# Token normalisation of both FFNs in a segment of its own, transposes through four PSUM banks, and a reset of buffer ages in the mixer

## The chip, the core and the metric

One NeuronCore of a Trainium2 chip runs the whole block for 1024 tokens of width 1024 in float32. The metric is device microseconds of one execution; before the change the median of three runs is 2161.04 us (2158.54 to 2163.19). The engines are TensorE (PE, with its weight loads as PEld), VectorE (DVE), ScalarE (ACT), GpSimd (POOL) and SyncE, whose queue SP issues the DMAs.

## What is computed

```python
x = x + 0.5 * swiglu_ffn(x, ffn1_norm, ...)      # d_ff = 2816
h = rms_norm(x, mix_norm); P = h @ w_in          # 4944 columns
ya = dsa_attention(...)                          # indexer scores, top 256 keys, softmax
yb = mlstm_branch(...)                           # causal conv, chunkwise scan
x = x + (sigmoid(ga) * (ya @ w_proj_a) + sigmoid(gb) * (yb @ w_proj_b)) @ w_out
x = x + 0.5 * swiglu_ffn(x, ffn2_norm, ...)

def swiglu_ffn(x, g, w_gate, w_up, w_down):
    h = rms_norm(x, g)
    return (silu(h @ w_gate) * (h @ w_up)) @ w_down
```

## The kernel before

**Products.** Every float32 operand is split into a high and a low part, and each product is three matmuls (`mm3`, lines 658 to 660). The gate and up projections use a seven-product scheme over 2x2 blocks (Strassen's form): the normalised, transposed tokens are combined into seven operands T0 to T6 of four 128x512 panels each (a high and a low part per panel), and the weight blocks are combined in the same way, on the fly, by `Pairs._prep` (lines 253 to 303: sums on DVE at L280 to L291, the high part on ACT at L297, the low part on DVE at L298). `gate_up` (line 911) walks 11 column pairs p and seven products q: first (0,0), (0,1), (1,0), (1,1), then the other five of p = 0 in the order 5, 4, 6, 2, 3, then all seven of each further p. One (p, q) is 24 matmuls of 512 columns: gate and up, four panels, three parts.

**The prologue.** `operands` (line 846) is a generator that makes T0 to T6; `gate_up` advances it just ahead of the product that needs the operand: T0 and T1 ahead of (0,0), T5 ahead of (0,1), T4 ahead of (1,0). It goes so:

- tokens 0 to 3 (128 each) are normalised by `norm` (line 759): a square with row sum on ACT into a scratch buffer (L763), a scale on DVE (L664), a power on POOL (L665), a multiplication on DVE (L765) into a buffer `xn`;
- for k = 0 to 7, `turned` (line 769) transposes column block k of the four tokens into one PSUM bank (four PE transposes, L773), and `put_turned` (line 835) reads the bank three times: high part on ACT (L841), low part on DVE (L842), a plain copy on ACT (L844) into one of four buffers `b1`. This gives T0 (k = 0 to 3) and T1 (k = 4 to 7);
- the four `xn` buffers are freed; tokens 4 to 7 are normalised in place; eight more `turned` calls (each read once by ACT, L878) and DVE subtractions (L879, L880) give T5, then T4 (`put2`, `split`: L790, L791), T6 (L894), T2 and T3 (L905).

**Buffers.** SBUF is cut into segments of 1024-column pages with the program's own allocator: a `Segment` tracks 64-column units, an `Arena` chooses among segments. `find` (line 89) takes, among free places, the one freed longest ago (the highest `freed` mark in it is the lowest of all), or the lowest address when `keep` is set. A buffer that was freed in program order may still be read on the chip; its next writer then waits for that reader. Scratch buffers, `xn`, `b1`, the early weights (two pages in total) and evicted results all come from the arena `ar`, in an FFN the segments `plain` (nine pages) and `more` (two). `segment(tag, ...)` (line 621) replaces a segment by a fresh one, whose first writer waits for all users of the old one. The segment `h0` (eight pages) is empty at the start of both FFNs until T5 and T4 are put there.

**PSUM.** Eight banks. `psA` gives banks 0 and 1, `psB` (line 605) alternates between 2 and 3, `psS` alternates between the pairs 4-5 and 6-7. `turned` takes its bank from `psB`. `turned` is also used by the mixer's `late_tokens` and `early_tokens` (lines 1050 and 1073).

**Order.** The code's order gives priorities; the framework's planner then fixes one order per engine from modelled durations, and on the chip each engine runs its list in that order. The second FFN follows `merge` (line 2079), whose last step `accumulate` (line 794) finishes the tokens one by one: 24 matmuls per token (L805 to L809), then the residual addition on DVE (L810). The second FFN's normalisation of a token can begin when that is done. The mixer lies between the FFNs, from about 640 to 1491 us: projections (pumped between other work), indexer scores, top-k (`topk`, a background generator), the mLSTM, attention and the merge. Its buffers come from the same arena, first with `plain`, later with `more`, `extra`, `spare` and `rawx`.

Of the kernel before, what the change touches and what calls it, by code (L numbers as in the profile page):

```python
# [59 lines left out]
class Buf:  # L60
# [4 lines left out]
    def __init__(self, seg, off, n):  # L65
        self.seg, self.off, self.n = seg, off, n
        self.f = seg.t[:, off:off + n]
        self.r = self.f.bitcast(F32R)
# [509 lines left out]
class Block:  # L578
    def __init__(self, tc, pools, a):
        self.tc, self.nc, self.a = tc, tc.nc, a  # L580
        self.sb, self.ps, self.dr = pools
        self.ar, self.rr, self.own = Arena(), Arena(), {}
        self.plain("plain", "more")
        self.round("round", "spare", "extra")
        for t in ("raw", "rawx", "side"):
            self.segment(t, None)
        self.whole_raw = True
        self.w = Weights(self, 0, 0)
        self.bg = ()
        self.due = [0, 0]  # L590

        self.psum = self.ps.tile([P, 4096], F32, name="psum", bufs=1)
        self.turn, self.turnB, self.turnS = 0, 2, 4
        self.last = None


# [24 lines left out]
    def segment(self, tag, arena):  # L621

        old = self.own.pop(tag, None)
        if old:
            assert not any(old.used), tag
            for a in (self.ar, self.rr):
                if old in a.segs:
                    a.segs.remove(old)
        self.own[tag] = Segment(self.sb, tag, PAGES[tag])
        if arena:  # L630
            arena.segs.append(self.own[tag])

    def close(self, tag):

        for a in (self.ar, self.rr):
            if self.own[tag] in a.segs:
                a.segs.remove(self.own[tag])
# [130 lines left out]

    def turned(self, xn, k):

        ps = self.psB()
        for i in range(4):
            self.nc.tensor.transpose(ps[:, i * P:(i + 1) * P], xn[i].f[:, k * P:(k + 1) * P], self.ident)  # L773
        return ps
# [47 lines left out]
    def put(self, q, j, src, tag):  # L822

        hi, lo = self.take(tag, 512), self.take(tag, 512)
        self.split(hi.r, lo.r, src)
        self.T[q][j] = (hi, lo)

    def put2(self, q, i, src, tag):

        hi, lo = self.take(tag, 1024), self.take(tag, 1024)  # L830
        self.split(hi.r, lo.r, src)
        for j in range(2):
            self.T[q][2 * i + j] = hi.part(j * 512, 512), lo.part(j * 512, 512)
# [12 lines left out]
    def operands(self, xs, gain, spill=None):  # L846


        nc, ar, v = self.nc, self.ar, self.nc.vector
        T = self.T = {q: [None] * 4 for q in range(7)}  # L850
        put, put2 = self.put, self.put2
        xn = []
        for t in range(4):
            n = ar.alloc(1024)
            self.norm(xs[t], n)
            xn.append(n)
        if spill:
            for t in range(8):
                spill(t)
        b1 = [ar.alloc(1024) for _ in range(4)]  # L860
        for k in range(8):
            self.put_turned(k // 4, k % 4, xn, k, gain, "swap", b1[k // 2].f[:, k % 2 * 512:k % 2 * 512 + 512])
            if k == 3:
                yield 0
        for n in xn:
            n.free()
        yield 1
        for t in range(4, 8):
            self.norm(xs[t], xs[t])
        b11, b21 = b1[:2], b1[2:]  # L870
        t1, t2, b22 = [], [], []
        for i in range(2):
            two = [self.take("side", 1024) for _ in range(2)]
            n = ar.alloc(1024)
            for j in (2 * i, 2 * i + 1):
                c = slice(j % 2 * 512, j % 2 * 512 + 512)
                for b, k in zip(two, (j, 4 + j)):
                    nc.scalar.activation(b.f[:, c], self.turned(xs[4:8], k), AF.Copy, scale=gain[:, k:k + 1])  # L878
                v.tensor_tensor(two[0].f[:, c], two[0].f[:, c], b11[i].f[:, c], ALU.subtract)  # L879
                v.tensor_tensor(n.f[:, c], two[1].f[:, c], two[0].f[:, c], ALU.subtract)  # L880
                put(5, j, n.f[:, c], "h0")
            t1.append(two[0])
            b22.append(two[1])
            t2.append(n)
        yield 5
        for i in range(2):
            put2(4, i, t1[i].f, "h0")
            t1[i].free()
        yield 4
        for x in xs:  # L890
            x.free()
        self.segment("h1", None)
        for i in range(2):
            v.tensor_tensor(b11[i].f, t2[i].f, b11[i].f, ALU.subtract)  # L894
            put2(6, i, b11[i].f, "h1")
            b11[i].free()
        yield 6
        for i in range(2):
            put2(2, i, b22[i].f, "h1")
            b22[i].free()  # L900
        yield 2
        self.segment("side", None)

        for i in range(2):
            v.tensor_tensor(b21[i].f, b21[i].f, t2[i].f, ALU.subtract)  # L905
            put2(3, i, b21[i].f, "side")
            b21[i].free()
            t2[i].free()
        yield 3
# [139 lines left out]

    def late_tokens(self, xs, spill):  # L1050

        nc, v, gain = self.nc, self.nc.vector, self.g_mix
        self.segment("h1", None)
        self.segment("side", None)
        self.T = {q: [None] * 4 for q in range(7)}
        for t in range(4, 8):
            spill(t)
            self.norm(xs[t], xs[t])
        self.b12, self.b22 = [], []
        for i in range(2):  # L1060
            b12, b22 = self.take("side", 1024), self.take("side", 1024)
            for j in (2 * i, 2 * i + 1):
                c = slice(j % 2 * 512, j % 2 * 512 + 512)
                self.put_turned(2, j, xs[4:8], 4 + j, gain, "h1", b22.f[:, c])
                nc.scalar.activation(b12.f[:, c], self.turned(xs[4:8], j), AF.Copy, scale=gain[:, j:j + 1])
            n = self.ar.alloc(1024)
            v.tensor_tensor(n.f, b22.f, b12.f, ALU.subtract)
            self.put2(6, i, n.f, "h1")
            n.free()
            self.b12.append(b12)  # L1070
            self.b22.append(b22)
# [1041 lines left out]
    def run(self, x, out):  # L2113
        nc, ar = self.nc, self.ar
# [81 lines left out]
            self.close(t)  # L2196
        self.pump_past((GATES[2], 3))
        self.plain("more", "extra", "spare")
        self.staged(self.gates())
        self.bg = [self.topk(js, share) for js, share in zip(((2, 3, 4, 5), (6, 7)), self.tk)]  # L2200
        self.mlstm_begin()
# [28 lines left out]
            nc.sync.dma_start(xs[t].f, d_x[t])  # L2230
        pairs = Pairs(self, a["ffn2_w_gate"][0], a["ffn2_w_up"][0])
        self.merge(yaT, xs, pairs)
        self.segment("side", None)
        self.segment("h0", None)
        self.segment("swap", None)
# [49 lines left out]
```

## Time and profile before

| | us |
|---|---|
| median of 3 runs | 2161.04 |
| the profiled execution, whole | 2156.2 |
| its span in the profile | 2154.5 |
| PE busy in the span | 2067.5 (96%) |
| DVE busy | 1632.2 (76%) |
| ACT busy | 1040.8 (48%) |
| POOL busy | 381.2 (18%) |

Times in the profile count from the start of the span. "Idle before" is the time in which an engine stood still ahead of an instruction, with the engine, buffer and line that released it. PEclk is the granted TensorE clock as a share of full speed: 1.00 is 2.4 GHz, 0.50 is 1.2 GHz. A busy PE is not PE at its peak: matmuls overlap, and at half clock a slow matmul counts as busy too, so the pitch from start to start is what tells PE's speed.

### The profile page before, as it was taken

To read this page: it belongs to the slowest core of one execution; us is meant where nothing else is said; L and a number is where in the kernel's file an instruction comes from. 1 tells how busy PE (TensorE), PEld (TensorE's weight loads), DVE (VectorE), ACT (ScalarE), POOL (GpSimd) and SP (SyncE) were. 2 spreads that over 40 slices of the span, in tenths; PEclk is the share of its full clock that TensorE was granted. 3 is DMA by queue.
4 is the path that set the end of the run, shared out by engine and by line. 5 is a ranking of instruction groups with operands and counts; after the bars stand their busy time and mean duration, and the time that the engine had idled before them with its cause. 6 is when DMAs were issued, how large, how long until landed. Compare 5 with 4: busy or idle time off the path is not lost.

```text
span 2154.5 us, 27729 instructions
## 1 busy us (share of the span) xinstructions
PE 2067.5 (96%) x9397; PEld 1686.8 (78%) x9397; DVE 1632.2 (76%) x2806; ACT 1040.8 (48%) x1928; POOL 381.2 (18%) x391
## 2 busy tenths in 40 slices
PE   6999999999999999999998999899899999999999
PEld 5788787888887778677777787777688888888887
DVE  6987887678855885988899689665786667669964
ACT  7332233344446664965885578323633333334442
POOL 1000000000303224434445545221000000000300
PEclk9999999999999999999999999999899999999999
DMA  5379994393522324456775222612243333277341
GB/s 181 124 245 291 280 289 153 132 364 125 168 68 92 90 72 120 133 167 178 226 224 164 93 74 70 249 59 88 68 143 108 105 101 113 98 258 276 96 142 40
DMA packets 275466, 326.76 MB, mean 152 GB/s; under 512 B 20236, under 2 KB 185724, under 8 KB 275324
## 3 DMA queue, kind: packets, MB, share of 16 engines
q1 hardware_dynamic: 275324, 324.99, 46.5%
q8 instruction: 74, 1.21, 0.2%
q14 instruction: 68, 0.56, 0.1%
HBM read 224.23 MB, written 100.70 MB: 151 GB/s over the span
## 4 chain that ended last, share of the span: by engine, by line
PE 45%; DVE 10%; ACT 3%; DMA 2%; issue 2%; POOL 0%; SPq 0%; DVEq 0%; ACTq 0%; POOLq 0%
PE psum L658 12%; PE psum L660 12%; PE psum L659 12%; PE psum L1983 1%; DVE plain L1476 1%; PE psum L805 1%; PE psum L809 1%; PE psum L807 1%; DVE h L791 1%; PE psum L1365 1%; PE psum L2038 1%; PE psum L2037 1%; PE psum L1366 1%; ACT plain L1502 0%; ACT round L408 0%
## 5 line engine op out<-in xcount | busy, mean ns | idle before, releaser
L658 PE MATMUL psum<-h,round 128*128 128x512 f32 x656 | 261.8, 400 | 4.2 <-DVE plain L976 1.6
L659 PE MATMUL psum<-h,round 128*128 128x512 f32 x656 | 259.5, 396 | 1.1 <-DVE h L791 0.8
L660 PE MATMUL psum<-h,round 128*128 128x512 f32 x656 | 259.1, 395 | 0.3 <-DVE round L298 0.3
L545 POOL TENSOR_TENSOR swap<-swap,h 128x1024 f32<-128x1024 f32 x12 | 32.9, 2773 | 1014.8 <-DVE h L531 1014.8
L409 POOL TENSOR_TENSOR round<-raw,round 128x512 fp32r<-128x512 f32 x108 | 149.4, 1392 | 155.7 <-ACT round L408 122.1
L658 PEld LDWEIGHTS psum<-h,round 128*128 128x128 f32 x656 | 124.3, 190 | 33.9 <-DVE plain L976 2.0
L660 PEld LDWEIGHTS psum<-h,round 128*128 128x128 f32 x656 | 123.9, 189 | 27.9 <-issue 1.8
L659 PEld LDWEIGHTS psum<-h,round 128*128 128x128 f32 x656 | 124.2, 189 | 26.9 <-DVE h L791 1.3
L658 PE MATMUL psum<-swap,round 128*128 128x512 f32 x328 | 131.6, 406 | 9.9 <-ACT plain L1452 2.6
L660 PE MATMUL psum<-swap,round 128*128 128x512 f32 x328 | 129.9, 397 | 1.2 <-POOL round L409 1.2
L659 PE MATMUL psum<-swap,round 128*128 128x512 f32 x328 | 130.5, 398 | 0.1
L1476 DVE TENSOR_SCALAR_CACHE_REDUCE plain<-plain 128x384 bf16<-128x384 f32 (+1 forms) x124 | 100.3, 808 | 2.5
L297 ACT ACTIVATE round<-plain 128x512 fp32r<-128x512 f32 x75 | 46.8, 630 | 102.4 <-PE psum L659 80.6
L790 ACT ACTIVATE round<-plain 128x512 fp32r<-128x512 f32 x72 | 45.1, 631 | 102.2 <-PE psum L659 90.2
L658 PE MATMUL psum<-h,extra 128*128 128x512 f32 x200 | 80.2, 402 | 6.2 <-ACT h L790 4.9
L658 PEld LDWEIGHTS psum<-swap,round 128*128 128x128 f32 x328 | 63.2, 193 | 27.4 <-ACT plain L1452 3.0
L791 DVE TENSOR_TENSOR round<-plain,round 128x512 fp32r<-128x512 f32 x72 | 55.9, 780 | 37.6 <-ACT round L790 37.3
L408 ACT ACTIVATE round<-raw 128x512 fp32r<-128x512 f32 x108 | 66.4, 622 | 33.4 <-PE psum L659 20.6
L659 PE MATMUL psum<-h,extra 128*128 128x512 f32 x200 | 79.5, 397 | 2.2 <-DVE h L791 2.2
L658 PE MATMUL psum<-h,spare 128*128 128x512 f32 x200 | 78.8, 395 | 1.3 <-DVE plain L976 1.3
L660 PE MATMUL psum<-h,extra 128*128 128x512 f32 x200 | 79.0, 395 | 0.0
L659 PE MATMUL psum<-h,spare 128*128 128x512 f32 x200 | 78.4, 392 | 0.0
(753 smaller groups left out, 5972.5 us busy)
## 6 DMA issues: line engine op xcount, KB each, us to landing
plain<-d_a SPq DMA_DIRECT2D x154, 256.0 KB
d_a<-plain SPq DMA_DIRECT2D x131, 256.0 KB
raw<-in_ffn_w_gate_dram SPq DMA_DIRECT2D x44, 512.0 KB
raw<-d_s SPq DMA_DIRECT2D x74, 256.0 KB
h<-in_ffn_w_down_dram SPq DMA_DIRECT2D x66, 256.0 KB
plain<-in_w_in_dram SPq DMA_DIRECT2D x32, 512.0 KB
d_s<-plain SPq DMA_DIRECT2D x64, 256.0 KB
raw<-in_w_in_dram SPq DMA_DIRECT2D x53, 256.0 KB
```

The source lines that it names most:

```text
L297: k.nc.scalar.activation(hi.r.rearrange("p (k c) -> p k c", k=4), src, AF.Copy)
L408: self.done_A = k.nc.scalar.activation(hi.r, raw.f, AF.Copy).ins
L409: k.nc.gpsimd.tensor_tensor(lo.r, raw.f, hi.f, ALU.subtract)
L545: k.nc.gpsimd.tensor_tensor(x(th, dh), x(th, dh), u, ALU.add)
L658: mm(ps, lhs[0], rhs[0], start=start, stop=False, skip_group_check=more)
L659: mm(ps, lhs[0], rhs[1], start=False, stop=False, skip_group_check=more)
L660: mm(ps, lhs[1], rhs[0], start=False, stop=stop, skip_group_check=more)
L790: self.split_A = self.nc.scalar.activation(hi, src, AF.Copy).ins
L791: self.nc.vector.tensor_tensor(lo, src, hi.bitcast(F32), ALU.subtract)
L805: mm(ps[:, n:n + 512], ah, wh[:, n:n + 512], start=j == 0, stop=False)
L807: mm(ps[:, n:n + 512], ah, wl[:, n:n + 512], start=False, stop=False)
L1476: v.tensor_scalar(s.junk[:, :s.width[j]], s.sc[j], s.cand[:, j:j + 1], None, ALU.is_ge, ALU.add, accum_out=s.cnt[:, j:j + 1])
```

## The change

In both FFNs the four `xn` buffers come from `h0` instead of the arena, and `h0` is replaced by a fresh segment once they are freed. While the flag `wide` is set (from the start to the mixer's `late_tokens`, and again after `merge`), `turned` goes round banks 0 to 3 instead of 2 and 3. In the mixer, just ahead of the gates, the top-k and the mLSTM, `level()` sets the age mark of every unit of every segment to zero, so that `find` takes the first free place by address as long as there is one not used since. Nothing that is computed changes.

```diff
         self.psum = self.ps.tile([P, 4096], F32, name="psum", bufs=1)
-        self.turn, self.turnB, self.turnS = 0, 2, 4
+        self.turn, self.turnB, self.turnS, self.turnT = 0, 2, 4, 3
+        self.wide = True
         self.last = None
...
+    def level(self):
+
+        for s in self.own.values():
+            s.freed = [0] * len(s.freed)
...
     def turned(self, xn, k):
 
-        ps = self.psB()
+        if self.wide:
+            self.turnT = (self.turnT + 1) % 4
+            ps = self.bank(self.turnT)
+        else:
+            ps = self.psB()
...
         for t in range(4):
-            n = ar.alloc(1024)
+            n = self.take("h0", 1024)
             self.norm(xs[t], n)
             xn.append(n)
...
         for n in xn:
             n.free()
         yield 1
+        self.segment("h0", None)
         for t in range(4, 8):
             self.norm(xs[t], xs[t])
...
     def late_tokens(self, xs, spill):
 
+        self.wide = False
...
         self.pump_past((GATES[2], 3))
         self.plain("more", "extra", "spare")
+        self.level()
         self.staged(self.gates())
...
         self.merge(yaT, xs, pairs)
+        self.wide = True
         self.segment("side", None)
```

## Rows read from the trace of the kernel before

**Rows 1.** The page: the span, and the busy time of each engine.

```profile
span 2154.5 us, 27729 instructions
PE 2067.5 (96%) x9397; PEld 1686.8 (78%) x9397; DVE 1632.2 (76%) x2806; ACT 1040.8 (48%) x1928; POOL 381.2 (18%) x391
```

**Rows 2.** Windows: length, busy us (count) by engine, PEclk, DMA share, GB/s.

```profile
13.47:57.63 44.16, 38.27 (x164) 29.92 (x165) 33.15 (x53) 36.69 (x61) 3.56 (x4) 0.88 0.40 130
1491.59:1545.84 54.25, 42.50 (x170) 31.93 (x171) 33.12 (x52) 36.19 (x58) 4.11 (x5) 0.81 0.17 59
1540.00:1545.00 5.00, 4.40 (x10) 3.51 (x11) 5.00 (x7) 1.56 (x3) 0.00 (x0) 0.50 0.00 0
1650.00:1700.00 50.00, 50.00 (x222) 41.42 (x221) 33.81 (x54) 15.39 (x25) 0.00 (x0) 1.00 0.32 105
```

**Rows 3.** The same view of both prologues, transposes alone (L773; PE, PEld).

```profile
1491.59:1545.84 54.25, 10.99 (x58) 7.63 (x58) 0.81 0.17 59
13.47:57.63 44.16, 9.54 (x56) 7.69 (x56) 0.88 0.40 130
```

**Rows 4.** Timeline at the second FFN's start: start, us, what, [idle before <-releaser].

```profile
1482.96 1.22 DVE L810 SCALAR_TENSOR_TENSOR h<-psum,h 128x1024 f32<-128x1024 f32 x1 [0.87 <-PE psum L809]
...
1490.97 0.61 PE L809 MATMUL psum<-more,side 128*128 128x512 f32 x2
...
1491.67 1.06 ACT L763 ACTIVATE more<-h 128x1024 f32<-128x1024 f32 x1 [0.94 <-issue]
...
1494.48 0.65 PE L773 MATMUL psum<-ident,plain 128*128 128x128 f32 x2 [2.89 <-DVE plain L664]
...
1495.69 0.80 PE L658 MATMUL psum<-swap,round 128*128 128x512 f32 x1 [0.56 <-ACT swap L841]
...
1501.40 0.40 PE L659 MATMUL psum<-swap,round 128*128 128x512 f32 x1
...
1502.10 0.60 PE L773 MATMUL psum<-ident,plain 128*128 128x128 f32 x4
1502.46 0.48 PE L659 MATMUL psum<-swap,round 128*128 128x512 f32 x1
```

**Rows 5.** The same timeline, between the second FFN's two token halves.

```profile
1518.75 0.60 PE L773 MATMUL psum<-ident,plain 128*128 128x128 f32 x4
1519.06 1.06 ACT L763 ACTIVATE plain<-h 128x1024 f32<-128x1024 f32 x1 [4.04 <-PE psum L773]
...
1519.16 0.69 DVE L280 TENSOR_TENSOR plain<-raw 128x512 f32<-128x512 f32 x1 [4.88 <-PE psum L773]
...
1536.25 0.80 PE L658 MATMUL psum<-h,extra 128*128 128x512 f32 x1 [2.90 <-ACT h L790]
...
1540.60 0.80 PE L659 MATMUL psum<-h,extra 128*128 128x512 f32 x1 [2.19 <-DVE h L791]
```

**Rows 6.** DVE groups from 1494 to 1567 us: count, busy, mean ns, idle before.

```profile
L842 DVE SCALAR_TENSOR_TENSOR swap<-psum,par,swap 128x512 fp32r<-128x512 f32 x8 | 5.9, 749 | 14.1 <-ACT swap L841 14.1
```

**Rows 7.** The chain of waits, second FFN: start, us, what.

```profile
1544.63 4.43 DVE h L791 x5
...
1559.76 4.50 DMA rawx<-in_ffn_w_up_dram
```

**Rows 8.** Timeline of the first FFN's prologue.

```profile
32.67 1.06 ACT L763 ACTIVATE plain<-h 128x1024 f32<-128x1024 f32 x1 [0.81 <-PE psum L773]
...
44.02 1.97 PE L773 MATMUL psum<-ident,h 128*128 128x128 f32 x8 [2.39 <-ACT side L878]
```

**Rows 9.** Waits of PE on L878; then L844 by line: ns min/median/max.

```profile
PE psum L773 <- ACT side L878: 4.3, 6, 2.4
...
L844 ACT ACTIVATE plain<-psum,par x16: 672/689/730, 19.9 to 1513.7; 128x512 f32<-128x512 f32 x16
```

**Rows 10.** The mixer from 850 us: busy by engine, and PE's longest wait.

```profile
850.00:1450.00 600.00, 561.59 (x2760) 454.72 (x2761) 494.47 (x1082) 402.08 (x876) 260.66 (x275) 0.98 0.47 149
...
PE psum L2037 <- DVE h L1997: 6.4, 4, 2.8
```

## The prediction

> **What bounds the kernel now.** The page comes first [rows 1]: PE is busy for 2067.5 of 2154.5 us, so 87 us of idle PE is all that reordering can win, plus what PE loses while its clock is down. The windows say where that sits. In steady state (1650 to 1700 us) 222 matmuls take 50 us, a pitch of 0.225 us. The two prologues stand out [rows 2]. From 13.47 to 57.63 us PE finishes 164 instructions, from 1491.59 to 1545.84 us 170, at a mean clock of 0.88 and 0.81. Of these, 56 and 58 are transposes [rows 3], and four of those take 0.36 us of PE time when warm (1502.10 to 1502.46) [rows 4]. Without idling, at full clock, the first FFN's stretch would need 108 x 0.225 + 56 x 0.09 = 29.3 us of its 44.2, and the second's 112 x 0.225 + 58 x 0.09 = 30.4 us of its 54.25. So **14.9 and 23.8 us** are lost there, partly idle and partly at half clock.
>
> Then the timeline tells why. In the second FFN, three squares of tokens 5 to 7 are left to do when ACT stops for 4.04 us and DVE for 4.88 us, both released by the same thing: the transposes of k = 7, which PE does last, at 1518.75 [rows 5]. Their inputs are the `xn` buffers. While four pages of the arena hold `xn`, four hold `b1` and two the early weights, ten of eleven are taken; so the next scratch buffer for a square and the next one for weight sums are `xn` pages, freed in the code but still to be read by PE. Behind that wait everything for T5 is queued: squares, powers, transposes, ACT's copies, DVE's subtractions. PE runs out of products, waits 2.90 us for the high parts of T5 and 2.19 us for the low parts, and the granted clock falls to 0.50 (1.2 GHz) in 1540 to 1545 us [rows 2, 5]. The chain of waits runs through DVE from there on (1544.63: five L791 in a row), up to a weight load at 1559.76 [rows 7].
>
> **The change part by part.**
>
> *A, the second FFN's start.* Token 3's residual is finished at 1482.96 + 1.22 = 1484.2, but its square starts at 1491.67 [rows 4]: its scratch buffer lies in `more`, the fresh segment whose predecessor PE reads until the last matmul of the merge (1490.97 + 0.61). With `xn` in `h0` (last used for the merge's gates, long before) four more pages of `plain` are free and no scratch buffer needs `more`. Token 3 can then be normalised and transposed beside the merge's last tokens, with all four panels of T0 in four banks. The first product moves from 1495.69 to 1491.6: 4.1 us. PE also stays warm: the 13 matmuls from 1495.69 to 1501.40 take 5.71 us where 13 x 0.225 = 2.9 would do, 2.8 us more. Bounds 0 (token 3 still late) and 6.9; I take 6.9, since every row that makes it late names `more`.
>
> *B, the second FFN's T5.* The waits of 4.04 and 4.88 us go. The norms of tokens 5 to 7, three times a square, scale, power and multiplication, move beside the products of T0 and T1; no DMA is in them, POOL is busy for 4.1 of 54 us [rows 2], and what they pass on ACT and DVE are evictions and weight splits. DVE stood idle for 14.1 us ahead of its eight L842 [rows 6] and for 4.88 ahead of L280, 19 us into which later work can move. Bounds: 4.9 (that wait alone, the order after it unchanged) and 23.8 - 6.9 = 16.9 (PE never starves). DVE is late next: in 1540 to 1545 it is busy for all of 5.00 us [rows 2], so PE can't gain all. I take 9.5, somewhat under the middle.
>
> *C, the first FFN.* The same wait is shorter (0.81 us on ACT at 32.67), but PE again waits at 44.02 [rows 8], and DVE is idle for 11.0 of the 44.2 us [rows 2]. The tokens come from HBM and the start at 13.47 doesn't move. Bounds 0.8 and 11.0; I take 6, the middle.
>
> *D, the banks.* In the second half each bank is read once, and PE waited 4.3 us for banks behind L878, in both FFNs together [rows 9]. I count this within B and C. A copy of ACT lasts 0.69 us and there are two for each k of the first half, so ACT alone needs 8 x 1.38 = 11.0 us for T0 and T1. A rule speaks against this part: the Trainium skill, "PSUM — Partial Sum Buffer", section "PSUM bank collisions raise a hardware error", says that two engines must not touch one bank at once, so a bank's three readers go one after another; eight turns over two banks would be shorter than ACT's own work, and four banks would bring nothing. The sum by that rule would be 4.3 us less.
>
> *E, `level()` and moved buffers.* It issues no instruction. It and the changed history of `plain` give the mixer's buffers other places: a writer may meet a reader that is still busy, or miss one that it met before. PE idles for 38.4 us from 850 to 1450, and the largest wait that one cause makes there is 6.4 us [rows 10]. So I bound this by -6 and +6 and take 0. The new `h0` before T5 waits for the transposes of k = 7; on PE these precede T5's own, so it costs nothing unless PE's order were turned round, and then no more than B. The flag and bank numbers cost nothing.
>
> Sum: 6.9 + 9.5 + 6 + 0 = 22 us. The profiled execution is 2156.2 us and would become 2134; the median of the runs is 4.8 us above it, so **2139 us** is forecast.
>
> **The rivals.**
>
> *The planner or DVE keeps the order.* The lists are fixed from modelled times, and these put k = 7 as late as 1518.75. If work doesn't move up, only the named waits go: 4.1 us of A, 4.9 of B, 0.8 of C, 10 us in all, 2151. For it: the chain behind the wait is DVE's own [rows 7], in any order. Against it: 19 us of DVE idling ahead of that.
>
> *The prologues gain nothing.* If the last free page still turns out to be one that PE reads late (`b1` is read until T3), the wait moves to another buffer of the same arena, and the time stays at about 2161. Against it: four of eleven pages come free.
>
> *Slower: the mixer.* From the gates and top-k on, `level()` makes the allocator take the lowest address and not the place freed longest ago, so top-k, gates and mLSTM are put into pages that were freed just before. Each such meeting can cost what one cost in the FFN, 4.9 us on DVE. To overturn 22 us and be slower by over 0.2%, PE's idle time there must grow by 22 + 4.3 = 26 us, from 38 to 64: five or six such meetings, all reaching PE. DVE is busy for 494 of the 600 us, so lost DVE time does count. It would give some 2168 us. Against it: the age zero holds for each place once only.
>
> *The mixer gains too.* Packed buffers leave larger free pieces, top-k's last step finds its two buffers sooner, and PE's longest waits shrink: 6 us or more on top of PE's bounds in A to C, 2122 or below.
>
> **How the numbers follow.** Forecast, both prologues close by 12 to 34 us with the mixer within 6: 0.66. Order kept, about 10 us: 0.17. No gain: 0.05. Slower through the mixer: 0.08. Mixer gains as well: 0.04. About 0.2% (4.3 us) is what a measurement can tell from no change. So faster is 0.66 + 0.17 + 0.04 = 0.87, same 0.05, slower 0.08. The bounds add up to 6.9 + 16.9 + 11 + 6 = 41 us at the good end, 2120; the range goes from 2122 to 2155, that is to gains of 39 and 6 us: it takes in most of the second case and leaves out no gain, slower, and the tails.
>
> **What would show it.** In the changed profile: token 3's square starts before 1491 us less the first FFN's gain, and PE's idle time and low clock between the merge and the first product vanish (A); no square of tokens 5 to 7 and no L280 is released by L773, and T5's products start less than 3 us after the last product of T1, at clock 1.00 (B); the first FFN's second column pair starts some 6 us sooner (C); the mixer's length is the same within 6 us (E). The forecast is wrong if DVE still has long gaps ahead of L842, or if the mixer is longer by over 10 us.

## The result and the profile after

The changed kernel takes 2138.49 us (median of four runs, 2137.93 to 2143.08), the kernel before 2160.48 in four runs on the same chip. The ratio is 0.9902 [0.9884, 0.992]: 22.0 us faster, where 2139.0 us had been forecast. The profiled execution is 2138.81 us with a span of 2136.9.

The page of the kernel after, as in [rows 1]. Most lines have moved down: L763 is now L769, L773 is L783, L658 to L660 are L664 to L666, L790 and L791 are L800 and L801, L842 is L852, L878 is L889 (L890 in the kernels that split the change by flags).

```profile
span 2136.9 us, 27748 instructions
PE 2056.9 (96%) x9397; PEld 1682.9 (79%) x9397; DVE 1637.5 (77%) x2806; ACT 1037.7 (49%) x1928; POOL 381.0 (18%) x391
```

PE executes the same 9397 matmuls and is busy for 10.6 us less; the mean granted clock is 0.993, where it was 0.988. Windows of the two prologues, columns as in [rows 2]. The first is the first FFN's old stretch; the second goes from the merge's last matmul to T5's first product; the third goes on from there.

```profile
13.47:57.63 44.16, 41.40 (x191) 32.38 (x191) 40.31 (x61) 38.16 (x63) 2.96 (x4) 1.00 0.41 134
...
1492.87:1519.92 27.05, 27.05 (x144) 22.77 (x144) 22.23 (x35) 23.85 (x41) 2.68 (x2) 1.00 0.20 71
1519.92:1542.00 22.08, 20.16 (x84) 15.20 (x83) 21.98 (x30) 11.66 (x16) 0.00 (x0) 1.00 0.29 89
```

In the first FFN's 44.16 us PE finishes 191 instructions where it finished 164, at clock 1.00 where it was 0.88. In the second FFN PE does not idle at all until T5 begins, and the granted clock there is 1.00, that is 2.4 GHz (before, 0.81 in the mean of 1491.59 to 1545.84 [rows 2]). Then DVE is the bound: 21.98 of 22.08 us. The timeline of the second FFN's start, columns as in [rows 4]:

```profile
1481.63 1.06 ACT L769 ACTIVATE plain<-h 128x1024 f32<-128x1024 f32 x1 [1.35 <-DVE h L820]
...
1487.82 1.06 ACT L769 ACTIVATE plain<-h 128x1024 f32<-128x1024 f32 x1 [2.05 <-DVE h L820]
...
1489.51 0.60 PE L783 MATMUL psum<-ident,h 128*128 128x128 f32 x4
...
1492.25 0.62 PE L819 MATMUL psum<-more,side 128*128 128x512 f32 x2
1492.70 0.39 PE L664 MATMUL psum<-swap,round 128*128 128x512 f32 x1
...
1492.63 1.08 ACT L769 ACTIVATE plain<-h 128x1024 f32<-128x1024 f32 x1
...
1498.90 1.05 ACT L769 ACTIVATE plain<-h 128x1024 f32<-128x1024 f32 x1
...
1519.92 0.39 PE L664 MATMUL psum<-h,round 128*128 128x512 f32 x1
...
1525.05 0.50 PE L665 MATMUL psum<-h,extra 128*128 128x512 f32 x1 [0.51 <-DVE h L801]
```

Token 3's square (1481.63) lies in `plain` and runs eleven microseconds before the merge ends, where in [rows 4] it waited for that end in `more`. The transposes of T0 run between the merge's own products (1489.51), and the first product follows the merge's last matmul without a gap. The squares of tokens 5 to 7 (1487.82, 1492.63, 1498.90) no longer wait for any transpose. T5's first product comes 27.05 us behind the merge; before, 44.66 us (1491.59 to 1536.25 [rows 5]).

Where the time came from, as stretches of the two profiled executions (the mixer from its first square to the merge's last matmul):

| stretch | before, us | after, us | difference |
|---|---|---|---|
| start to mixer | 637.9 | 636.1 | -1.8 |
| of it to the parameter transposes behind the first column pair | 80.5 | 73.3 | -7.2 |
| mixer | 853.7 | 856.8 | +3.1 |
| merge's end to end of span | 662.9 | 644.0 | -18.9 |

That adds up to 17.6 us, the difference of the spans. The before's profile reaches the mixer early for its code: six kernels here whose first FFN is that of the kernel before reach it at 637.9 to 643.2 us, at 641.1 in the mean, so the first FFN's gain is 1.8 us against this one execution and nearer 6 us against the mean (two kernels with the new first FFN: 636.1 and 634.3). With a spread of 5 us for one and the same code, the 6 is good to a few microseconds. Six, less 3, plus 19 is the 22 us of the medians.

### The profile page after: what moved, and what is told of

The parts are those of the page before. It is cut to its first block, busy times and chain, and to the rows that moved or that the text cites. A ratio compares the mean times of both kernels' runs of the same rounds, so it can differ in the third digit from the quotient of the medians.

```text
span 2136.9 us, 27748 instructions
## 1 busy us (share of the span) xinstructions
PE 2056.9 (96%) x9397; PEld 1682.9 (79%) x9397; DVE 1637.5 (77%) x2806; ACT 1037.7 (49%) x1928; POOL 381.0 (18%) x391
## 4 chain that ended last, share of the span: by engine, by line
PE 64%; DVE 16%; DMA 7%; ACT 4%; issue 3%; SPq 0%; POOL 0%; DVEq 0%; ACTq 0%; POOLq 0%
PE psum L664 18%; PE psum L665 18%; PE psum L666 18%; DMA plain<-in_w_in_dram 2%; DVE plain L1488 2%; PE psum L1377 1%; DMA d_s<-plain 1%; PE psum L1378 1%; PE psum L1995 1%; PE psum L815 1%; PE psum L817 1%; PE psum L819 1%; DVE h L801 1%; PE psum L2050 1%; PE psum L2049 1%
## 5 line engine op out<-in xcount | busy, mean ns | idle before, releaser
L664 PE MATMUL psum<-h,round 128*128 128x512 f32 x656 | 263.7, 403 | 7.5 <-DVE plain L987 4.0
L666 PE MATMUL psum<-h,round 128*128 128x512 f32 x656 | 260.3, 397 | 1.5 <-DVE round L298 0.9
L664 PEld LDWEIGHTS psum<-h,round 128*128 128x128 f32 x656 | 125.0, 191 | 37.6 <-DVE plain L987 4.8
L666 PEld LDWEIGHTS psum<-h,round 128*128 128x128 f32 x656 | 125.0, 191 | 29.7 <-POOL round L409 1.5
L664 PE MATMUL psum<-swap,round 128*128 128x512 f32 x328 | 131.1, 401 | 13.8 <-ACT round L408 3.7
L666 PE MATMUL psum<-swap,round 128*128 128x512 f32 x328 | 129.8, 397 | 0.2 <-POOL round L409 0.2
L800 ACT ACTIVATE round<-plain 128x512 fp32r<-128x512 f32 x72 | 45.1, 631 | 102.8 <-PE psum L665 96.7
L664 PEld LDWEIGHTS psum<-swap,round 128*128 128x128 f32 x328 | 62.7, 191 | 32.0 <-ACT round L408 6.4
L801 DVE TENSOR_TENSOR round<-plain,round 128x512 fp32r<-128x512 f32 x72 | 55.8, 779 | 37.4 <-ACT round L800 37.1
L408 ACT ACTIVATE round<-raw 128x512 fp32r<-128x512 f32 x108 | 66.8, 623 | 29.8 <-PE psum L665 17.0
L664 PE MATMUL psum<-h,extra 128*128 128x512 f32 x200 | 78.1, 391 | 2.6 <-DVE more L987 1.5
L664 PE MATMUL psum<-h,spare 128*128 128x512 f32 x200 | 78.3, 394 | 2.1 <-DVE plain L987 1.6
L665 PE MATMUL psum<-h,spare 128*128 128x512 f32 x200 | 78.1, 391 | 1.9 <-DVE h L801 1.9
L665 PE MATMUL psum<-h,extra 128*128 128x512 f32 x200 | 78.0, 390 | 0.5 <-DVE h L801 0.5
L666 PE MATMUL psum<-h,spare 128*128 128x512 f32 x200 | 77.9, 390 | 0.0
```

Source lines behind the costliest of these rows:

```text
L408: self.done_A = k.nc.scalar.activation(hi.r, raw.f, AF.Copy).ins
L664: mm(ps, lhs[0], rhs[0], start=start, stop=False, skip_group_check=more)
L665: mm(ps, lhs[0], rhs[1], start=False, stop=False, skip_group_check=more)
L666: mm(ps, lhs[1], rhs[0], start=False, stop=stop, skip_group_check=more)
L800: self.split_A = self.nc.scalar.activation(hi, src, AF.Copy).ins
L801: self.nc.vector.tensor_tensor(lo, src, hi.bitcast(F32), ALU.subtract)
```

## The experiments

Each ratio is against the kernel before on the same chip (medians 2159.26, 2158.35 and 2157.82 us on the three chips). The kernels split the change by two flags, `wide` (four banks) and `own_xn` (the segment), set at the start for the first FFN and behind `merge` for the second:

```diff
-        self.wide = True
+        self.wide, self.own_xn = False, False
...
-            n = self.take("h0", 1024)
+            n = self.take("h0", 1024) if self.own_xn else ar.alloc(1024)
...
-        self.segment("h0", None)
+        if self.own_xn:
+            self.segment("h0", None)
```

### The second FFN alone, and its two halves

All three leave `level()` out and the first FFN as before. Behind the merge they set:

```diff
-        self.wide = True
+        self.wide, self.own_xn = True, True      # f2_both
+        self.wide, self.own_xn = False, True     # f2_h0
+        self.wide, self.own_xn = True, False     # f2_banks
```

> Only the second FFN gets its own segment and four banks; the first FFN, the mixer and the allocator's ages are as before. Theory 1 (the whole gain of the change comes from the second FFN; what the first FFN wins is lost again in it): 18 us faster than before, 2143 where before has 2161, with the merge's end at 1491.6 to 1492.9 us as in the profiles of before and after. Theory 2 (the first FFN's 6 us reach the end and the mixer loses as much through level()): the second FFN alone gives more than the whole change, 22 us or more. Rival (both FFNs give half): 10 to 12 us.

> As f2_both, but transposes stay in two banks. If the buffers are the cause and the banks bind little (ACT's two copies per bank are longer than the turn of two banks): 15 to 18 us faster than before. If the banks carry a good part, as the 4.3 us of PE waiting on L878 suggest: 12 to 14 us faster. If the first operand's four panels in four banks carry the whole of the start: 9 to 11 us.

> Four banks in the second FFN, the tokens' buffers from the arena as before. Theory: token 3's scratch buffer still lies in the replaced segment and the squares of tokens 5 to 7 still wait for the last transposes, so 0 to 4 us faster; these transposes come somewhat earlier. If the banks are what matters: 10 us or more.

Times, and three points of the profile counted from the merge's last matmul:

| kernel | median us | ratio | first product | T5's first product | end of span |
|---|---|---|---|---|---|
| before | | | +4.10 | +44.66 | +662.9 |
| f2_h0 | 2154.03 | 0.9975 [0.9963, 0.9986] | -0.17 | +39.56 | +656.5 |
| f2_banks | 2146.87 | 0.9937 [0.9922, 0.9952] | +4.14 | +34.03 | +651.3 |
| f2_both | 2141.85 | 0.9923 [0.9905, 0.9941] | -0.17 | +27.05 | +643.4 |

From the merge's end to the end of the span the two halves add up: 6.4 and 11.6 us to 18.0, both together 19.5. In the medians f2_h0 gains 5.2 us, less than any of its three expectations, and f2_banks 12.4, where 0 to 4 was expected and 10 or more only "if the banks are what matters". The segment brings the start forward by 4.3 us, and T5 by 5.1, hardly more. The banks leave the start where it was and bring T5 forward by 10.6. The rows say why. The timeline of f2_h0 (the segment, two banks):

```profile
1491.18 1.06 ACT L769 ACTIVATE plain<-h 128x1024 f32<-128x1024 f32 x1 [1.84 <-DVE h L820]
...
1494.64 1.06 ACT L769 ACTIVATE plain<-h 128x1024 f32<-128x1024 f32 x1
...
1498.34 1.03 PE L783 MATMUL psum<-ident,h 128*128 128x128 f32 x8
...
1498.97 1.27 ACT L851 ACTIVATE swap<-psum,par 128x512 fp32r<-128x512 f32 x2 [1.51 <-PE psum L783]
...
1501.97 1.40 DVE L852 SCALAR_TENSOR_TENSOR swap<-psum,par,swap 128x512 fp32r<-128x512 f32 x2
...
1502.74 1.34 ACT L854 ACTIVATE plain<-psum,par 128x512 f32<-128x512 f32 x2 [1.47 <-DVE swap L852]
...
1507.45 1.04 PE L783 MATMUL psum<-ident,h 128*128 128x128 f32 x8
...
1517.53 1.03 PE L783 MATMUL psum<-ident,h 128*128 128x128 f32 x8
...
1528.30 5.08 PE L783 MATMUL psum<-ident,h 128*128 128x128 f32 x24 [2.78 <-ACT side L890]
...
1535.34 0.63 PE L664 MATMUL psum<-h,round 128*128 128x512 f32 x1 [1.96 <-ACT h L800]
```

Two squares of tokens 5 to 7 are done by 1495.7 and the third starts at 1500.13, 26 to 32 us sooner against the merge's end than before, and it helps nobody: the transposes of T5 stand in PE's list behind those of k = 7, and with two banks these come in pairs, k = 2 and 3 at 1498.34, 4 and 5 at 1507.45, 6 and 7 at 1517.53. A turn of the pair takes 9.1 us (1498.34 to 1507.45). Its reads are 1.27 + 1.40 + 1.34 us, but with what ACT and DVE do between them they end at 1504.08, 5.7 us after the transposes began; the other 3.4 us PE's own list adds, which has products in front of the next pair. In that turn PE stands still for nothing, a bank least of all: its list simply holds 36 long matmuls between the two pairs. In the next turn it holds 24, and PE waits 1.81 us for ACT's high part, not for a bank. So the two banks act through the order that the planner fixed beforehand, and hardly through waits on the chip. Whether another order would do as well with two banks was not tried. The timeline of f2_banks (four banks, `xn` in the arena as before):

```profile
1497.45 1.12 PE L783 MATMUL psum<-ident,plain 128*128 128x128 f32 x4 [2.89 <-DVE plain L670]
...
1506.79 1.91 PE L783 MATMUL psum<-ident,plain 128*128 128x128 f32 x16
...
1509.15 1.07 ACT L769 ACTIVATE plain<-h 128x1024 f32<-128x1024 f32 x1
...
1528.59 0.39 PE L664 MATMUL psum<-h,round 128*128 128x512 f32 x1
```

All four blocks of T1 are transposed in one go, 12.2 us behind the merge, where k = 7 came at 27.2 before (1518.75 [rows 5]). With that the `xn` pages are free too, and the square that waited until 1519.06, 27.5 us behind the merge, runs at 1509.15, 14.6 us behind it: **the buffer wait of [rows 5] ends early although no buffer has moved.** The groups of DVE for its eight L852 show what each half does to DVE's idle time ahead of them: 14.1 us before [rows 6], then f2_h0, f2_banks and the kernel after:

```profile
L852 DVE SCALAR_TENSOR_TENSOR swap<-psum,par,swap 128x512 fp32r<-128x512 f32 x8 | 5.7, 744 | 7.5 <-ACT swap L851 7.5
```
```profile
L852 DVE SCALAR_TENSOR_TENSOR swap<-psum,par,swap 128x512 fp32r<-128x512 f32 x8 | 5.7, 744 | 7.3 <-ACT swap L851 7.3
```
```profile
L852 DVE SCALAR_TENSOR_TENSOR swap<-psum,par,swap 128x512 fp32r<-128x512 f32 x8 | 5.6, 744 | 0.4 <-ACT swap L851 0.4
```

### Is it really `more` that makes the second FFN start late?

f2_both, with nothing but token 3's scratch buffer put back into `more`:

```diff
-            self.norm(xs[t], n)
+            self.norm(xs[t], n, "more" if self.own_xn and t == 3 else None)
```

> As f2_both, but token 3's square in the second FFN writes its scratch values into the replaced segment, as before. If that segment is why the second FFN starts late: the square waits for the merge's last matmul again, the first product comes 4.1 us after the merge's end instead of at once, and all of A is lost, 5 to 7 us slower than f2_both; T5 and the rest keep their gain. If the start comes from the banks or the tokens' segment in another way: within 1 us of f2_both.

2148.63 us, 0.996 [0.9946, 0.9974], with 6.8 us more than f2_both from the merge's end to the end of the span (650.2 to 643.4).

```profile
1497.96 1.06 ACT L769 ACTIVATE more<-h 128x1024 f32<-128x1024 f32 x1 [0.95 <-PE psum L819]
...
1504.04 1.11 PE L783 MATMUL psum<-ident,h 128*128 128x128 f32 x4 [6.17 <-DVE h L771]
1505.29 0.80 PE L664 MATMUL psum<-swap,round 128*128 128x512 f32 x1
```

The square is released by the merge's last matmul (L819), as in [rows 4], PE stands for 6.17 us, and the first product comes 7.42 us behind the merge. That is 3.3 us later than the 4.10 of before, so the 6.8 us are an upper bound of the price; that the segment delays the start is shown.

### The first FFN, and `level()` by itself

The second FFN is as before in all four. f1_level has the first FFN's segment and four banks with `level()`; f1_h0 the segment and `level()`; f1_banks the banks and `level()`; level_only neither. The first FFN's part without `level()` was not tried, so what follows on the segment holds beside `level()`.

```diff
-        self.wide = True
+        self.wide, self.own_xn = True, True      # f1_level
+        self.wide, self.own_xn = False, True     # f1_h0
+        self.wide, self.own_xn = True, False     # f1_banks
+        self.wide, self.own_xn = False, False    # level_only
```

> The change in the first FFN and level(), with the second FFN as before. Theory 1: 7 us ahead at the first column pair's end (73 instead of 80.5 us), 2 us ahead at the mixer's start (636 instead of 638), level with before at the merge's end, so within 3 us of before in all. Theory 2 (the first FFN's gain is real and lasts): 6 us faster.

> Before, with level() alone. Nothing ahead of the gates moves: the score phase ends at 809.5 us as before. If the mixer's buffers matter little: within 3 us of before. If level() is what costs the mixer its 2 to 3 us: 2 to 3 us slower. If it is what keeps the mixer from losing more: 0 to 5 us faster.

> The first FFN with its own segment for the tokens but two banks, and level(); the second FFN as before. By the second FFN, where the segment alone gave nothing behind the start, and since the first FFN's start hangs on the loads: the first column pair ends at 80 to 81 us as before (f1_level 73.1). If the buffers matter here: 76 or sooner.

> The first FFN with four banks but the tokens' buffers from the arena, and level(); the second FFN as before. By the second FFN, where four banks alone brought T5 forward by 10.6 us: the first column pair ends at 75 to 77 us, most of the 7.9 us that both parts give. If the squares of tokens 5 to 7 still wait for the last transposes long enough: 79 or later.

| kernel | median us | ratio | first pair's end | mixer starts | mixer's length |
|---|---|---|---|---|---|
| before | | | 80.5 | 637.9 | 853.7 |
| f1_level | 2157.47 | 0.9993 [0.9983, 1.0004] | 73.1 | 634.3 | 858.9 |
| f1_h0 | 2160.9 | 1.0018 [1.0009, 1.0027] | 81.1 | 639.8 | 860.4 |
| f1_banks | 2145.83 | 0.9952 [0.9938, 0.9966] | 77.3 | 633.7 | 847.3 |
| level_only | 2151.7 | 0.9974 [0.9964, 0.9984] | 81.0 | 641.7 | 847.5 |

In the prologue the pattern is the second FFN's: the segment alone brings nothing, the banks alone some 3.5 us, both together 7.5 (the first pair ends at 80.4 to 81.6 us in the six executions with the old first FFN). The transposes of PE in the kernel after and in f1_h0 (L783; f1_h0's next blocks come singly, at 23.01, 25.30, 32.82 and 36.02):

```profile
20.62 0.60 PE L783 MATMUL psum<-ident,h 128*128 128x128 f32 x4
22.00 1.47 PE L783 MATMUL psum<-ident,h 128*128 128x128 f32 x12
```
```profile
17.90 1.05 PE L783 MATMUL psum<-ident,h 128*128 128x128 f32 x4
19.95 0.60 PE L783 MATMUL psum<-ident,h 128*128 128x128 f32 x4
```

But the last column weighs as much. Five kernels with the mixer's code and the first FFN of the kernel before (it, f2_both, f2_h0, f2_banks, f2_more3) have a mixer of 852.4 to 856.7 us, 854.2 in the mean. `level()` alone shortens it by 6.7, more than any of its expectations had, and with the new segment in the first FFN it is 11 to 13 us longer than that, with the banks (858.9) or without them (860.4). So most of f1_level's 6.8 us at the mixer's start is lost in the mixer, and f1_banks owes as much of its 12 us to the mixer as to the first FFN.

The difference arises all along the mixer, most of it by the end of the top-k. Two marks divide it: the top-k's last step, on ACT, and the fourth and last of attention's copies of keys, on DVE:

| kernel | mixer's start to top-k's last step | to the fourth copy | to the merge's end |
|---|---|---|---|
| before | 517.0 | 38.8 | 297.9 |
| level_only | 513.6 | 47.6 | 286.3 |
| f1_banks | 513.7 | 47.6 | 286.0 |
| after | 518.7 | 48.8 | 289.3 |
| f1_level | 521.8 | 48.1 | 289.0 |
| f1_h0 | 522.5 | 49.9 | 288.0 |

With the segment, 5 to 9 of the 9 to 13 us are lost by the first mark. (In the kernel before the four copies stand elsewhere among PE's products, so its last two columns compare only as a sum.) The *first* copy would mislead: after the top-k's last step it comes in 42.1 us in the kernel after and in 30.2 in level_only, but in level_only the four copies are spread over 17.4 us, and over 6.7 in the kernel after. Windows of the whole mixer, after and then level_only:

```profile
636.10:1492.87 856.77, 805.47 (x3876) 654.01 (x3875) 681.48 (x1341) 547.34 (x1109) 337.73 (x338) 0.99 0.42 134
```
```profile
641.70:1489.19 847.49, 802.80 (x3865) 652.81 (x3863) 670.34 (x1334) 542.36 (x1099) 334.96 (x335) 0.98 0.43 135
```

PE is idle for 51.3 us in the first and 44.7 in the second. Two stalls of the mixer's background products stand near the top-k's last step (1154.8):

```profile
1143.84 0.50 PE L664 MATMUL psum<-swap,round 128*128 128x512 f32 x1 [3.54 <-ACT round L408]
...
1160.54 0.47 PE L664 MATMUL psum<-swap,round 128*128 128x512 f32 x1 [3.42 <-DVE more L1162]
```

From 1100 to 1200 us f1_level and f1_h0 show the same two waits, of 3.6 and 3.5 us for L408 and 2.5 and 3.4 for a sum in `more`. level_only and f1_banks show neither, but others (the longest 4.4 and 2.6 us, for a sum in `plain`); the kernel before has 1.7 us for L408 and 1.1 for another sum in `more`. So the two waits go with the segment in the first FFN, but they don't account for the loss.

One more thing differs. Compared by line and shape, the engines' lists in the mixer are the same in level_only and f1_banks, the same in f1_level, f1_h0 and the kernel after, and the same in the kernel before, f2_both, f2_h0, f2_banks and f2_more3; their mixers take 847.3 to 847.5, 856.8 to 860.4 and 852.4 to 856.7 us. From one of these groups to another the planner's order changes too: some 830 of PE's 3730 matmuls stand elsewhere in f1_level than in level_only. So a buffer's place works through new waits and through a new order, and these runs do not separate the two. Which moved buffer it is was not isolated either.

### Does the first FFN lose its lead to the loads of the mixer's weights?

Behind the first pair the lead shrinks from 7 us to some 6, and PE idles for 7.3 us from 82 to 350 us in the kernel after (3.5 before). In that stretch the DMA engines are 82% busy, loading the FFN's weights and, on the side, the mixer's `w_in`. One theory was that the loads are the bound. Three kernels skip every third call of the side work; a fourth gives each load one more call of time before its sums.

```diff
-            if p > 1 and beside:
+            if p > 1 and beside and n % 3 != 2:   # before_paced, after_paced, f2_both_paced
...
                     nc.sync.dma_start(two[h].f.rearrange("p (k c) -> p k c", k=4), src)
             yield
+            yield                                 # after_late
```

> Before, with the mixer's weight sums (loads of w_in and stores of d_s beside the first FFN) advanced at two of three products instead of at each, so that the same 38 loads and 76 stores are spread over more of the gate and up projections. Theory 1 (that stretch is bound by DMA, which is 0.94 busy from 150 to 330 us and 0.28 busy from 350 to 400): PE's idle time of 3.8 us there shrinks to under 1, the mixer starts about 3 us sooner. Rival (the idle time there comes from DVE alone): no change at the mixer's start.

> After, with the same pacing. Theory 1 (the first FFN's 7 us are lost because the stretch behind it is bound by DMA and ends at 327 us in both kernels): the first FFN keeps its lead, the mixer starts at 630 to 632 us instead of 636.1, and the whole is about 5 us faster than after if the mixer keeps its length. Rival (the lead is lost to DVE): the mixer's start stays within 1.5 us of 636.

> The second FFN's part of the change with the pacing, without level() and with the first FFN's prologue as before. If pacing is worth 3 us on before: 3 us faster than f2_both, about 2140. It moves the ages of the mixer's buffers too, so 4 us either way are possible there.

> After, with the weight sums' additions one product later behind their loads, so that DVE doesn't stand still for a load that hasn't landed. If PE's idle time of 7 us from 82 to 350 us comes from DVE standing behind loads of w_in (20 us in the profile of after), it falls under 3 us and the mixer starts at 630 to 633 us; the whole is 3 to 5 us faster if the mixer keeps its length, which moved buffers may change by 6 to 10 us either way. Rival (the loads and stores themselves hold PE's data back): mixer's start within 1.5 us of 636.

| kernel | median us | ratio | mixer starts | mixer's length |
|---|---|---|---|---|
| before_paced | 2174.94 | 1.0077 [1.0059, 1.0094] | 643.2 | 863.2 |
| f2_both_paced | 2155.27 | 0.9988 [0.9975, 1.0001] | 645.9 | 860.9 |
| after_paced | 2127.32 | 0.986 [0.9845, 0.9876] | 636.7 | 845.1 |
| after_late | 2146.64 | 0.9953 [0.9937, 0.9969] | 638.4 | 865.5 |

The windows from 82 to 350 us, of the kernel after, after_paced and after_late:

```profile
82.00:350.00 268.00, 260.69 (x1138) 214.01 (x1137) 219.32 (x360) 79.15 (x137) 0.00 (x0) 0.99 0.82 256
```
```profile
82.00:350.00 268.00, 263.28 (x1159) 217.08 (x1158) 208.98 (x339) 82.04 (x140) 0.00 (x0) 1.00 0.71 221
```
```profile
82.00:350.00 268.00, 263.14 (x1148) 215.86 (x1147) 206.66 (x337) 78.35 (x135) 0.00 (x0) 0.99 0.70 214
```

The DMA share falls from 0.82 to 0.71 and 0.70, and PE's idle time from 7.3 to 4.7 and 4.9 us. But the side work then goes on into 350 to 450 us, where PE, never idle in the kernel after, now is for 3.8 and 4.2 us:

```profile
350.00:450.00 100.00, 100.00 (x442) 82.78 (x442) 61.03 (x96) 29.98 (x49) 0.00 (x0) 1.00 0.48 167
```
```profile
350.00:450.00 100.00, 96.17 (x416) 78.77 (x416) 70.45 (x115) 26.93 (x46) 0.00 (x0) 0.98 0.77 246
```
```profile
350.00:450.00 100.00, 95.82 (x421) 78.66 (x421) 71.51 (x117) 29.23 (x50) 0.00 (x0) 1.00 0.81 264
```

The mixer starts no sooner (636.7 and 638.4, after 636.1), where 630 to 633 was expected; each is one execution, and the same code spreads over 5 us there. So the theory fell as far as it was tested: lowering the DMA engines' share from 0.82 to 0.70 in that stretch did not bring the first FFN's end forward. The idle time moves with the side work, whichever of its loads, sums and buffers it is that makes it. What makes these four totals differ by 48 us is, beside the parts of the two FFNs, the length of the mixer again, 845 to 866 us. **after_paced is the fastest kernel of all**, 11 us below the changed one. Its mixer is 11.7 us shorter than that of the kernel after and the rest is level, so it owes its lead to the mixer, and not to what its edit was meant to do; what shortens the mixer there (places of buffers, the lists' order) was not isolated. The same edit made the kernel before 17 us slower, and f2_both_paced has little left of f2_both's gain (0.9988, after 0.9923), where 3 us more had been expected.

## Why the prediction was right

**A, the second FFN's start, 6.9 us:** right. The start moved by 4.27 us where 4.1 was read, PE's clock is 1.00 from there on, and f2_more3 shows the reason given, `more`. Its price is less sharp: the segment alone gains 6.4 us (f2_h0), but moves the norms too, and f2_more3 loses 6.8, with a later start than before. The four banks that A counts on for T0 were not needed: f2_h0 starts as early with two.

**B, T5, 9.5 us between 4.9 and 16.9:** the size is near, 18.9 - 6.4 = 12.5 us, and DVE is the next bound, as expected. **The step that failed is the cause:** "Behind that wait everything for T5 is queued", and with the wait gone the norms were to move up and T5 with them. With the wait gone and two banks (f2_h0), the norms did move up, by over 20 us, and T5 came 5.1 us sooner, of which the start gives 4.3. The wait was real, but it only marked where the transposes of k = 7 stood, and these were late because of the banks, through their place in PE's list.

**D, the banks, counted within B and C; without them 4.3 us less:** this fell with it. Four banks alone, with all buffers where they were, gain 11.6 of the second FFN's 18.9 us, and without them the first FFN gains nothing. The bound was taken from what PE was seen to wait for, and from readers' durations: 8 x 1.38 us of ACT. The turn of a bank was 9.1 us in f2_h0, with 4.0 us of reads in it for the pair. The rest is the place of each step in three in-order lists, PE's above all, with 36 long matmuls between two pairs of transposes. The rule of the Trainium skill ("PSUM — Partial Sum Buffer", section "PSUM bank collisions raise a hardware error") is not touched by this: the first bank's readers do go one after another here, 1498.97, 1501.97 and 1502.74, and the last waits for DVE, whose result it does not read. The inference drawn from it, that more banks bring nothing, was wrong, since it priced a turn by its readers alone.

**C, the first FFN, 6 us:** right in size, 7.2 us at the first pair and about 6 at the mixer's start; wrong in its cause in the same way as B ("The same wait is shorter"): f1_h0 has the segment and none of the gain. The segment is even a loss there: f1_banks gains 12.0 us on the kernel before and f1_level, which differs by the segment in the first FFN, 1.8. By these two the change without that segment would be some 10 us faster, an estimate; it was not run.

**E, the mixer, 0 within 6 us:** +3 in the change, inside its bounds. But two effects hide in it: `level()` gains 6.7, the segment in the first FFN loses 9 to 13 (after, f1_level and f1_h0 against level_only). Over all kernels the mixer is 845 to 866 us long; a bound of 6 us was too narrow for a part of the change by itself.

Of the rivals, "the planner or DVE keeps the order" (10 us) comes nearest to f2_h0, that is the change without its banks: for this FFN it gives 4.1 + 4.9 = 9.0 us, 6.4 was measured, and although the norms moved up, the transposes of T5 hardly did. "The mixer gains too" has the size of level_only, 6.7 us; its reason, the top-k's two buffers, is not shown. "Slower: the mixer" names the right stage, but the price is 9 to 13 us and not 26, and it comes with the first FFN's segment; `level()` by itself makes the mixer shorter. The total came out close partly by luck: the second FFN gave 18.9 us where A and B make 16.4, the mixer took 3 back, and B's and D's prices were put into one sum. Had the banks been left out of the second FFN, the same argument would have forecast about 12 to 16 us for it (A and B, with or without D's 4.3), and 6.4 was measured.

## What to carry to other kernels

A wait for a buffer names the instruction that freed it; before crediting the buffer, ask why that instruction was late. Where transposes share an in-order list with long products, two PSUM banks can cost far more than their readers' durations, as here, by whole turns of the list: count the turns and what stands between them, and split banks and buffers into separate runs. And when an edit changes what an allocator has seen, compare stage by stage from fixed points, since stages that the edit never touched move by 10 us.

## What was not expected

Other places of buffers, with the other order of the lists that comes with them, move an 850 us stage by 13 us at the same instructions: 847.5 us in level_only, 860.4 in f1_h0. And the same lists at the start of the program reach the mixer at 637.9 to 643.2 us in six executions (one each of six kernels), so a difference of a few microseconds there cannot be read from one pair of profiles.
